# A two-layer hybrid decoder trunk on one core: first weights on another queue, and the outputs of four attention heads one step later

## The chip, the core and the metric

The kernel runs on one core of one Trainium2 chip. Its engines work side by side, each on its own list of instructions in a fixed order: TensorE (PE) multiplies matrices, VectorE (DVE) and ScalarE (ACT) work on elements, and GpSimd (POOL) has almost nothing to do here. Transfers (DMAs) are started by an instruction on the queue of one engine. In the kernel before, nearly all of them stand on SyncE (SP). An instruction waits until what it reads is there and until what it overwrites has been read; everything behind it on its engine waits with it.

The metric is the time of one execution in microseconds (us). The kernel before took 1193.77 us, the median of three runs (1192.67 to 1194.18).

## What is computed

The reference takes x, 512 tokens of width 1024, in float32, through two layers. The change touches the first layer's attention alone, which is this, cut to what matters:

```
proj = rms_norm(x) @ w_in                       # q, k, v of 8 dilated heads and 4 differential heads
qa, ka, qb, kb = rms_norm(each head) * gain
oa = dilated_mixture_attention(qa, ka, va)      # 8 heads of 64, causal, with a bias by distance

# differential: two softmaxes per head, v of width 128
p = softmax(q @ k.T * 64**-0.5 - slope * distance)      # c = 0, 1, causal
attn = p[:, :, 0] - lam * p[:, :, 1]
ob = rms_norm(attn @ v, b_sub_norm) * (1 - lam_init)
x += concat(oa, ob) @ w_out
```

A causal convolution with a gated unit follows each layer's mixer, and the second layer's mixer is a gated linear recurrence. The changed kernel does not touch these.

## The kernel before, in words

**Products.** Every product is made of three matmuls, since each float32 operand is split into a rounded part and the rest: for weights `wh` (cast on ACT, line 104) and `wl` (subtraction on DVE, line 106), for activations `xh` and `xl` (lines 231 and 233).

**Attention as eight tiles.** The queries, keys and values of layer 0 come in eight tiles of 384 columns, tile n = 0 to 7 in the order of `ORDER`: n = 0 to 3 are the four differential heads (`attn_b`), n = 4 to 7 are pairs of dilated heads (`attn_a`). One tile's projection is 16 groups of six matmuls: four units u of weights, and in each unit four blocks b of 128 tokens (`group`, lines 348 to 350). A unit of weights is cast on ACT and subtracted on DVE into one of four buffers, two units ahead, so a cast waits until PE has last read what stood in its buffer.

**The order of the work is written by hand.** `line` holds the groups of all tiles, one after the other, and behind them 32 short steps of the output projection (`early_out`). The attention of tile n is cut into steps, and `PLACES` says behind which group each stands, counted from the end of the tile's own projection: `qk` (transposes of q and k, line 414), `sc` (scores in three batches: blocks 0 and 1, block 2, block 3, line 447), `tr` (transposes of the softmaxed rows, line 468), `out` (attention times v, lines 481 to 491) and, for the differential heads, `norm`. `LAST` does the same for the last tile. Place 27.3 stands behind the eleventh group of the tile after next, so the output of one head falls into the scores of the next. PE keeps this order exactly (`pe`). The order on ACT, DVE and SP is made by a scheduler from the program's dependences.

**The output of a differential head.** `out` (lines 567 to 576) is twelve matmuls into the bank `O`, a copy of it to `ob` (ACT, line 571), its square `obsq` (ACT, line 573), and the split of the square into `obh` (ACT, line 126) and `obl` (DVE, line 127). `norm` (lines 578 to 593) multiplies both by a matrix of 1/128 (PE, lines 129 and 130, tile `obms`), which gives the mean of the squares, and works out the normalised output. The rows of the next head's softmax run on the same two engines: line 458 on DVE (an operation of the tensor and the bias with a running minimum), line 461 on ACT (the exponential), and line 556 on ACT (the scaling by the row's sum, line 515 in a dilated head).

**The start.** `first_tile` loads four pairs of x and weights, each transfer on SP's queue (lines 306 and 307), the first pair in two halves. ACT makes `xh`, then `wh`; DVE makes `xl`, then `wl`; then PE starts. Behind these transfers SP loads the other parameters (line 308), the next weights (line 113) and three tables of distances (`dist_a`, `lnc`, `dist_b`, lines 257 to 259), from which DVE makes the heads' biases (line 432).

Of the kernel before, what the change touches and what calls it, by code (L numbers as in the profile page):

```python
# [12 lines left out]
F32 = mybir.dt.float32  # L13
# [6 lines left out]
P = 128  # L20
S = 512
# [6 lines left out]
NT = 8  # L28

ORDER = (4, 5, 6, 7, 0, 1, 2, 3)  # L30


BATCHES = ((0, 1), (2,), (3,))
PLACES = dict(qk=9, sc=(12, 14, 16), tr=(18.5, 20.7, 23.5, 25.2), step=1, out=27.3, norm=29)
LAST = dict(qk=7.5, sc=(9.8, 10.5, 11.2), tr=(12.7, 13.4, 14.2, 15), step=0.35, out=16.2, norm=18)

OUT_GROUP = 0.65
# [25 lines left out]
def trunk(  # L63
# [15 lines left out]
    nc = tc.nc  # L79
    V, A, T, G = nc.vector, nc.scalar, nc.tensor, nc.gpsimd  # L80
# [13 lines left out]
    def nm(s):  # L94
        uid[0] += 1
        return f"{s}{uid[0]}"

    def bank(s):
        return pa.tile([P, S], F32, tag="pa", name=nm(s))
# [119 lines left out]
    with ExitStack() as actx:  # L219
        ap1 = actx.enter_context(tc.tile_pool(name="ap1", bufs=1))  # L220
        ap2 = actx.enter_context(tc.tile_pool(name="ap2", bufs=2))
        smp = actx.enter_context(tc.tile_pool(name="smp", bufs=2))
# [4 lines left out]
        def x_split(raw, cs):  # L227
            for c in cs:
                src = raw[:, (c % 2) * S : (c % 2 + 1) * S]
                hi = xp.tile([P, S], F32R, tag=f"xh{c}", name=nm("xh"))  # L230
                last = A.activation(hi, src, AF.Copy, scale=col(C_ATTN_G + c))
                lo = xp.tile([P, S], F32R, tag=f"xl{c}", name=nm("xl"))
                V.scalar_tensor_tensor(lo, src, col(C_ATTN_G + c), hi.bitcast(F32), ALU.mult, ALU.subtract)
                xs.append((hi, lo))
            return last
# [62 lines left out]
        def first_tile():  # L298


            xr = [ap2.tile([P, 13 * P], F32, tag=("pth", "ptl")[u % 2], name=nm("xr"))[:, : 2 * S] for u in range(4)]
            wr = [rawp.tile([P, 2 * CW], F32, tag="raw", name=nm("raw")) for u in range(4)]
            for u in range(4):
                for j in range(2 if u == 0 else 1):
                    cx, cw = (slice(j * S, (j + 1) * S), slice(j * CW, (j + 1) * CW)) if u == 0 else (slice(None),) * 2
                    nc.sync.dma_start(xr[u][:, cx], xT[u][:, cx])
                    nc.sync.dma_start(wr[u][:, cw], w_att[ORDER[0], u][:, cw])
            nc.sync.dma_start(pt[:, KC:], par[:, KC:])
            units = []
            for u in range(4):  # L310
                if u:
                    x_split(xr[u], (2 * u, 2 * u + 1))
                    units.append(split(wr[u], 2 * CW))
                    with tc.issue_after(last.ins):
                        x_square(xr[u - 1], (2 * u - 2, 2 * u - 1))
                    continue
                wh = whp.tile([P, 2 * CW], F32R, tag="wh", name=nm("wh"))
                wl = wlp.tile([P, 2 * CW], F32R, tag="wl", name=nm("wl"))
                for j in range(2):
                    cw = slice(j * CW, (j + 1) * CW)  # L320
                    last = x_split(xr[0], (j,))
                    with tc.issue_after(last.ins):
                        last = A.copy(wh[:, cw], wr[0][:, cw])  # L323
                    V.tensor_tensor(wl[:, cw], wr[0][:, cw], wh[:, cw].bitcast(F32), ALU.subtract)
                units.append((wh, wl))
            x_square(xr[3], (6, 7))
            return units
# [94 lines left out]
        oT = {}  # L422

        def where(n):
            return LAST if n == NT - 1 else PLACES

        def head_bias(h):
            bt = ap2.tile([P, S], F32, tag="bias", name=nm("bias"))
# [64 lines left out]
        def pt_tiles():  # L493
            return (ap2.tile([P, 13, P], F32R, tag="pth", name=nm("pth")),
                    ap2.tile([P, 13, P], F32R, tag="ptl", name=nm("ptl")))
# [46 lines left out]
        def attn_b(n):  # L542

            p = ORDER[n]
            st = {}

            def sc(blocks):
                if blocks[0] == 0:
                    st["b"] = head_bias(4 + p)
                rows = products(tiles[n]["qk"], blocks)  # L550
                for i in blocks:
                    for c in range(2):
                        st[i, c] = softmax_row(rows[c, i], i, st["b"])
                        if c == 0:
                            e0, r0 = st[i, 0]
                            A.activation(e0, e0, AF.Copy, scale=r0)
                        else:
                            (e0, _), (e1, r1) = st[i, 0], st[i, 1]
                            V.tensor_tensor(r1, r1, lam, ALU.mult)
                            V.scalar_tensor_tensor(e0, e1, r1, e0, ALU.mult, ALU.add)  # L560

            def tr(i):
                if i == 0:
                    st["pt"] = pt_tiles()
                transposed(st[i, 0][0], i, *st["pt"])

            def out():
                o_ps = bank("O")
                pv(o_ps, tiles[n]["v"], *st["pt"])
                st["o"] = smp.tile([P, S], F32, tag="sq", name=nm("ob"))  # L570
                A.copy(st["o"], o_ps)
                sq = smp.tile([P, S], F32, tag="sm3", name=nm("obsq"))
                A.activation(sq, o_ps, AF.Square)
                hi = smp.tile([P, S], F32R, tag="sq", name=nm("obh"))
                lo = smp.tile([P, S], F32R, tag="t", name=nm("obl"), bufs=1)
                st["ms"] = mean_rows("obms", hi, sq, lo)

            def norm():
                o = st["o"]
                ps, products_of = st["ms"]  # L580
                products_of(pe)
                y = smp.tile([P, S], F32, tag="sm3", name=nm("oby"))
                A.activation(y, ps, AF.Ln, bias=epsb)
                A.activation(y, y, AF.Exp, scale=-0.5)
                t = smp.tile([P, S], F32, tag="sq", name=nm("obt"))
                V.tensor_tensor(t, y, y, ALU.mult)
                V.scalar_tensor_tensor(t, ps, EPS, t, ALU.add, ALU.mult)
                V.tensor_scalar(t, t, -0.5 * (1.0 - LAM_INIT), 1.5 * (1.0 - LAM_INIT), ALU.mult, ALU.add)
                V.tensor_tensor(y, y, t, ALU.mult)
                V.scalar_tensor_tensor(o, o, col(C_BS), y, ALU.mult, ALU.mult)  # L590
                hi, lo = o_tiles(p)
                A.copy(hi, o)
                V.tensor_tensor(lo, o, hi.bitcast(F32), ALU.subtract)

            at = where(n)
            steps = [(g, partial(sc, b)) for g, b in zip(at["sc"], BATCHES)]
            steps += [(g, partial(tr, i)) for i, g in enumerate(at["tr"])]
            return steps + [(at["out"], out), (at["norm"], norm)]


# [376 lines left out]
```

## Time and profile before

| | before |
|---|---|
| median of three runs | 1193.77 us |
| the profiled execution | 1195.96 us |
| its span, first to last instruction | 1194.1 us |
| PE busy | 1181.2 us (99%) |
| DVE busy | 811.4 us (68%) |
| ACT busy | 585.6 us (49%) |
| granted TensorE clock, mean | 1.000 |

The page's span is 1.9 us shorter than the profiled execution, and that execution was 2.2 us above the median. The span is cut into 40 slices of 29.9 us on the page; layer 0's attention fills the first seven of them, up to about 230 us. PE is busy nearly without a gap, so what can be won or lost is what PE waits, and a wait is found by asking the trace what PE waited for, and then what the engine that it waited for was doing.

### The profile page before, as it was taken

The numbers are of one execution on the slowest core, as the hardware profiler recorded it, in microseconds if no ns is written. First come the engines' busy times: TensorE is split into PE (matmuls) and PEld (weight loads), VectorE is DVE, ScalarE is ACT, GpSimd is POOL, SyncE is SP. The second block draws the span as 40 slices with busy tenths as digits, with TensorE's granted clock in tenths as the row PEclk, the third lists the DMA queues.
The fourth block names the chain that finished last, engine by engine and source line by source line (L and its number), as shares of the span: only waits on it lengthen the run. The fifth ranks groups of instructions, "written<-read, shape, count | busy, mean of one in ns | idle before, by whom it ended". The sixth has DMA issues, their size and how long they took to land.

```text
span 1194.1 us, 14625 instructions
## 1 busy us (share of the span) xinstructions
PE 1181.2 (99%) x5566; PEld 990.6 (83%) x5566; DVE 811.4 (68%) x1327; ACT 585.6 (49%) x951; POOL 0.7 (0%) x6
## 2 busy tenths in 40 slices
PE   8999999999999999999999999999999999999998
PEld 8988888788888888888888878888888888888887
DVE  6977888688777763577436888668777763677431
ACT  6667788765444432344225688454444441444220
POOL 0000000000000000000000000000000000000000
PEclk9999999999999999999999999999999999999999
DMA  7221222062323232323233313323232323333221
GB/s 255 68 79 54 67 67 71 19 211 89 106 89 106 89 106 88 106 89 106 88 106 102 111 36 124 106 89 102 92 101 94 100 94 95 100 95 100 92 85 54
DMA packets 33910, 114.31 MB, mean 96 GB/s; under 512 B 3888, under 2 KB 4656, under 8 KB 33840
## 3 DMA queue, kind: packets, MB, share of 16 engines
q1 hardware_dynamic: 33552, 113.24, 29.8%
q8 instruction: 44, 0.72, 0.3%
q14 instruction: 26, 0.21, 0.1%
q10 hardware_dynamic: 288, 0.14, 0.0%
HBM read 111.27 MB, written 2.10 MB: 95 GB/s over the span
## 4 chain that ended last, share of the span: by engine, by line
PE 83%; ACT 3%; DVE 2%; issue 0%; DVEq 0%
PE mm L120 26%; PE mm L121 26%; PE mm L122 26%; ACT sm L461 1%; PE pj L348 1%; PE pj L350 1%; PE pj L349 1%; PE pt L468 1%; ACT sm L515 1%; PE S L447 0%; PE O L489 0%; DVE u L865 0%; DVE sm L458 0%; PE qkt L414 0%; DVE cv L708 0%
## 5 line engine op out<-in xcount | busy, mean ns | idle before, releaser
L104 ACT CAST wh<-raw 128x1024 fp32r<-128x1024 f32 (+1 forms) x207 | 211.1, 1021 | 285.8 <-PE mm L121 256.8
L122 PE MATMUL mm<-xh,wl 128*128 128x512 f32 x896 | 348.6, 389 | 0.0
L121 PE MATMUL mm<-xl,wh 128*128 128x512 f32 x896 | 348.6, 389 | 0.0
L120 PE MATMUL mm<-xh,wh 128*128 128x512 f32 x896 | 348.6, 389 | 0.0
L106 DVE TENSOR_TENSOR wl<-raw,wh 128x1024 fp32r<-128x1024 f32 (+1 forms) x207 | 244.8, 1184 | 43.0 <-ACT wh L104 39.4
L120 PEld LDWEIGHTS mm<-xh,wh 128*128 128x128 f32 x896 | 168.2, 188 | 35.0
L121 PEld LDWEIGHTS mm<-xl,wh 128*128 128x128 f32 x896 | 168.2, 188 | 35.0
L122 PEld LDWEIGHTS mm<-xh,wl 128*128 128x128 f32 x896 | 168.2, 188 | 34.9
L708 DVE SCALAR_TENSOR_TENSOR cv<-us,pt,cv 128x511 f32<-128x511 f32 (+2 forms) x216 | 160.5, 747 | 3.5
L120 PE MATMUL mm<-fh,wh 128*128 128x512 f32 x384 | 149.4, 389 | 0.0
L121 PE MATMUL mm<-fl,wh 128*128 128x512 f32 x384 | 149.4, 389 | 0.0
L122 PE MATMUL mm<-fh,wl 128*128 128x512 f32 x384 | 149.4, 389 | 0.0
L704 DVE TENSOR_TENSOR us<-mm,rs 128x512 f32<-128x512 f32 x104 | 71.6, 688 | 93.9 <-PE mm L122 93.6
L740 DVE TENSOR_TENSOR h<-mm,h 128x512 f32<-128x512 f32 (+1 forms) x49 | 33.2, 680 | 141.4 <-PE mm L122 141.4
L348 PE MATMUL pj<-wh,xh 128*128 128x384 f32 x256 | 92.7, 362 | 2.5 <-ACT wh L323 2.5
L729 ACT CAST fh<-cv 128x512 fp32r<-128x512 f32 x48 | 29.8, 621 | 126.4 <-DVE cv L726 126.4
L350 PE MATMUL pj<-wl,xh 128*128 128x384 f32 x256 | 87.2, 341 | 0.0
L349 PE MATMUL pj<-wh,xl 128*128 128x384 f32 x256 | 87.2, 341 | 0.0
L706 ACT ACTIVATE cv<-us,pt 128x512 f32<-128x512 f32 x104 | 84.3, 813 | 0.9 <-DVE us L704 0.6
L120 PEld LDWEIGHTS mm<-fh,wh 128*128 128x128 f32 x384 | 72.1, 188 | 15.0
L122 PEld LDWEIGHTS mm<-fh,wl 128*128 128x128 f32 x384 | 72.1, 188 | 15.0
L121 PEld LDWEIGHTS mm<-fl,wh 128*128 128x128 f32 x384 | 72.1, 188 | 14.9
(202 smaller groups left out, 1238.6 us busy)
## 6 DMA issues: line engine op xcount, KB each, us to landing
raw<-in_w_up_dram SPq DMA_DIRECT2D x96, 512.0 KB, 3.5
raw<-in_w_dn_dram SPq DMA_DIRECT2D x48, 512.0 KB, 3.5
raw<-in_w_att_dram SPq DMA_DIRECT2D x31, 384.0 KB, 3.4
raw<-in_w_ri_dram SPq DMA_DIRECT2D x16, 512.0 KB, 3.5
raw<-in_w_ao_dram SPq DMA_DIRECT2D x8, 512.0 KB, 3.6
raw<-in_w_ro_dram SPq DMA_DIRECT2D x8, 512.0 KB, 3.5
raw<-in_xT_dram SPq DMA_DIRECT2D x4, 512.0 KB, 4.4
out_dram<-h SPq DMA_DIRECT2D x7, 256.0 KB, 2.0
```

Of the source, the lines that this page charges most:

```text
L104: A.copy(hi, src)
L106: V.tensor_tensor(lo, src, hi.bitcast(F32), ALU.subtract)
L120: order(T.matmul(out, wh, xh, start=first, stop=False))
L121: order(T.matmul(out, wh, xl, start=False, stop=False))
L122: return order(T.matmul(out, wl, xh, start=False, stop=last))
L348: pe(T.matmul(o, xs[k][0][:, tb], wh[:, cw], start=k == 0, stop=False))
L349: pe(T.matmul(o, xs[k][1][:, tb], wh[:, cw], start=False, stop=False))
L350: pe(T.matmul(o, xs[k][0][:, tb], wl[:, cw], start=False, stop=k == KC - 1))
L704: V.tensor_tensor(u, ps, state["rs"], ALU.mult)
L706: A.activation(c, u, AF.Identity, scale=col(wcol + (taps - 1) * stride), bias=col(bcol))
L708: V.scalar_tensor_tensor(c[:, d:], u[:, : S - d], col(wcol + (taps - 1 - d) * stride), c[:, d:], ALU.mult, ALU.add)
L740: V.tensor_tensor(h[m][:, t], ps[:, t], h[m][:, t], ALU.add)
```

## The change

It has four parts.

1. The weights of the first tile, five transfers, are issued on ACT's queue and not on SP's.
2. In `PLACES`, `out` goes from 27.3 to 28.4 and `norm` from 29 to 30.4: outputs of tiles n = 0 to 5 stand one group later, for the differential heads behind the first scores of the next head and not ahead of them. (The last `tr` goes from 25.2 to 25.5, which is behind the same group.)
3. The last but one tile (n = 6) gets places of its own, `LAST_BUT_ONE`, closer together, with its output at 24.6 and not at 27.3.
4. The tiles `obsq` and `oby` take other buffers: `obsq` the one of tag `o`, `oby` the one of tag `t`, where both stood in the two buffers of tag `sm3`, which are also those of the last block of the softmax.

```
-PLACES = dict(qk=9, sc=(12, 14, 16), tr=(18.5, 20.7, 23.5, 25.2), step=1, out=27.3, norm=29)
+PLACES = dict(qk=9, sc=(12, 14, 16), tr=(18.5, 20.7, 23.5, 25.5), step=1, out=28.4, norm=30.4)
+LAST_BUT_ONE = dict(qk=9, sc=(12, 13.7, 15.4), tr=(17.8, 19.6, 21.4, 23.2), step=0.8, out=24.6)
 LAST = dict(qk=7.5, sc=(9.8, 10.5, 11.2), tr=(12.7, 13.4, 14.2, 15), step=0.35, out=16.2, norm=18)
...
                     nc.sync.dma_start(xr[u][:, cx], xT[u][:, cx])
-                    nc.sync.dma_start(wr[u][:, cw], w_att[ORDER[0], u][:, cw])
+                    A.dma_start(wr[u][:, cw], w_att[ORDER[0], u][:, cw])
             nc.sync.dma_start(pt[:, KC:], par[:, KC:])
...
         def where(n):
-            return LAST if n == NT - 1 else PLACES
+            return {NT - 1: LAST, NT - 2: LAST_BUT_ONE}.get(n, PLACES)
...
                 A.copy(st["o"], o_ps)
-                sq = smp.tile([P, S], F32, tag="sm3", name=nm("obsq"))
+                sq = smp.tile([P, S], F32, tag="o", name=nm("obsq"), bufs=1)
                 A.activation(sq, o_ps, AF.Square)
...
                 products_of(pe)
-                y = smp.tile([P, S], F32, tag="sm3", name=nm("oby"))
+                y = smp.tile([P, S], F32, tag="t", name=nm("oby"), bufs=1)
                 A.activation(y, ps, AF.Ln, bias=epsb)
```

The inserted line shifts every later line of the changed kernel by one, so line 461 of the kernel before is line 462 there. The texts below use the numbers of the kernel before; the rows of the order after the change have the new ones.

**The first place is ACT at the start.** Before, its only transfer is that of the first eight columns of parameters.

```order
L160 DMA pt<-in_par_dram 128x8
L231 ACTIVATE xh_150<-xr_129,pt 128x512
L323 CAST wh_148<-raw_133 128x384
L231 ACTIVATE xh_156<-xr_129,pt 128x512
L323 CAST wh_148<-raw_133 128x384
```

With the change:

```order
L161 DMA pt<-in_par_dram 128x8
L308 DMA raw_133<-in_w_att_dram 128x384 x2
L308 DMA raw_134<-in_w_att_dram 128x768
L308 DMA raw_135<-in_w_att_dram 128x768
L308 DMA raw_136<-in_w_att_dram 128x768
L232 ACTIVATE xh_150<-xr_129,pt 128x512
L324 CAST wh_148<-raw_133 128x384
```

Five transfers stand ahead of the first `xh`. The program's waits give the fourth and the fifth of them one each: transfers report on eight counters in turn, and the ninth waits until the first one on its counter has landed. The fourth waits for the first half of x, the fifth for the parameters.

**The second place is DVE in the first tile,** where `wl_172` and `wl_190` are the weights of units 1 and 2, and `xl_182` and `xl_186` the activations of unit 2. Before:

```order
L106 TENSOR_TENSOR wl_172<-raw_134,wh_170 128x768
L245 TENSOR_TENSOR xacc_178<-xsq_174,xsq_176 128x512
L233 SCALAR_TENSOR_TENSOR xl_182<-xr_131,pt,xh_180 128x512
L233 SCALAR_TENSOR_TENSOR xl_186<-xr_131,pt,xh_184 128x512
L106 TENSOR_TENSOR wl_190<-raw_135,wh_188 128x768
```

With the change:

```order
L107 TENSOR_TENSOR wl_172<-raw_134,wh_170 128x768
L433 TENSOR_SCALAR bias_552<-dist_b 128x512
L246 TENSOR_TENSOR xacc_178<-xsq_174,xsq_176 128x512
L234 SCALAR_TENSOR_TENSOR xl_182<-xr_131,pt,xh_180 128x512
L234 SCALAR_TENSOR_TENSOR xl_186<-xr_131,pt,xh_184 128x512
L107 TENSOR_TENSOR wl_190<-raw_135,wh_188 128x768
```

The bias of the first head, which reads `dist_b` and stood 17 instructions further on, now stands ahead of unit 2. On SP the three tables moved up too: they stand right behind the parameters and ahead of the next tile's weights, and by the same eight counters the issue of `dist_b` waits until the weights of unit 1 have landed.

**The third place is ACT at the output of head n = 0,** in the scores of head n = 1; the outputs of n = 1 and 2 stand alike. Before:

```order
L571 COPY ob_849<-O_836 128x512
L573 ACTIVATE obsq_851<-O_836 128x512
L104 CAST wh_1039<-raw_1037 128x768
L126 CAST obh_853<-obsq_851 128x512
L461 ACTIVATE sm_880,sum_883<-sm_880,mx_881 128x128
L461 ACTIVATE sm_887,sum_890<-sm_887,mx_888 128x128
L366 COPY qkraw_922<-pj_706 128x256
L378 ACTIVATE v_923<-pj_706,rstd 128x128
L556 ACTIVATE sm_880<-sm_880,sum_883 128x128
```

With the change:

```order
L105 CAST wh_1039<-raw_1037 128x768
L462 ACTIVATE sm_858,sum_861<-sm_858,mx_859 128x128
L462 ACTIVATE sm_865,sum_868<-sm_865,mx_866 128x128
L557 ACTIVATE sm_858<-sm_858,sum_861 128x128
L462 ACTIVATE sm_873,sum_876<-sm_873,mx_874 128x256
L462 ACTIVATE sm_880,sum_883<-sm_880,mx_881 128x256
L557 ACTIVATE sm_873<-sm_873,sum_876 128x256
L572 COPY ob_901<-O_888 128x512
L574 ACTIVATE obsq_903<-O_888 128x512
L367 COPY qkraw_922<-pj_706 128x256
L379 ACTIVATE v_923<-pj_706,rstd 128x128
L127 CAST obh_905<-obsq_903 128x512
```

The cast of weights and six operations of the next head's first two blocks, which stood behind the split of the square, now stand ahead of the copy of the output. On PE the two `obms` matmuls stood one group behind the scores of blocks 0 and 1, with the output and one group ahead of these; now the scores come first, then the output, two groups, the scores of block 2, and `obms` right behind them. For the output of n = 3, which falls into the scores of a dilated pair, ACT has four scalings and not two ahead of `obh`, and a second pair of the copies of lines 366 and 378.

## Rows read from the trace of the kernel before

**Rows 1.** What PE waited for, over the whole span: total, times, longest.

```profile
PE O L483 <- DVE ptl L472: 2.6, 3, 1.0
PE pj L348 <- ACT wh L323: 2.5, 2, 2.3
...
PE pt L468 <- DVE o L531: 1.1, 2, 0.8
PE pt L468 <- DVE ptl L472: 1.0, 2, 0.8
```

**Rows 2.** Timeline of PE, first tile: start, duration, line, tiles, count, wait before and releaser.

```profile
8.95 0.69 PE L348 MATMUL pj<-wh,xh 128*128 128x384 f32 x1 [2.32 <-ACT wh L323]
...
19.32 0.33 PE L350 MATMUL pj<-wl,xh 128*128 128x384 f32 x1
```

**Rows 3.** Timeline of ACT at the start.

```profile
3.91 0.72 ACT L231 ACTIVATE xh<-xr,pt 128x512 fp32r<-128x512 f32 x1 [1.89 <-DMA pt<-in_par_dram]
...
8.39 0.51 ACT L323 CAST wh<-raw 128x384 fp32r<-128x384 f32 x1 [2.23 <-DMA raw<-in_w_att_dram]
...
10.93 0.81 ACT L104 CAST wh<-raw 128x768 fp32r<-128x768 f32 x1
```

**Rows 4.** Timeline of SP's queue: the issues of the transfers.

```profile
2.12 0.43 SPq L307 DMA_DIRECT2D raw<-in_w_att_dram  x1
...
16.88 0.43 SPq L259 DMA_DIRECT2D dist_b<-in_dist_dram  x1
```

**Rows 5.** Transfers issued in the first 20 us: count, KB each, median us to landing.

```profile
dist_b<-in_dist_dram SPq DMA_DIRECT2D x1, 256.0 KB, 3.8
```

**Rows 6.** Timeline of DVE in the first tile.

```profile
12.65 0.68 DVE L245 TENSOR_TENSOR xacc<-xsq,xsq 128x512 f32<-128x512 f32 x1
13.26 1.41 DVE L233 SCALAR_TENSOR_TENSOR xl<-xr,pt,xh 128x512 fp32r<-128x512 f32 x2
14.58 0.95 DVE L106 TENSOR_TENSOR wl<-raw,wh 128x768 fp32r<-128x768 f32 x1
```

**Rows 7.** Timeline of PE at the output of head n = 1, and of tile 6's last scores.

```profile
86.98 0.40 PE L482 MATMUL O<-pth,v 128*128 128x512 f32 x1
88.33 0.50 PE L483 MATMUL O<-ptl,v 128*128 128x512 f32 x1 [0.95 <-DVE ptl L472]
...
91.27 0.33 PE L447 MATMUL S<-qh,qh 64*128 64x128 f32 x2
...
93.71 0.50 PE L130 MATMUL obms<-obl,ones_r 128*128 128x512 f32 x1
...
217.89 0.45 PE L447 MATMUL S<-qh,qh 64*128 64x384 f32 x2
...
218.62 0.50 PE L120 MATMUL mm<-oh,wh 128*128 128x512 f32 x1
```

**Rows 8.** Timeline of ACT at the output of head n = 1.

```profile
90.26 0.59 ACT L571 COPY ob<-O 128x512 f32<-128x512 f32 x1 [4.32 <-PE O L484]
...
91.23 0.83 ACT L104 CAST wh<-raw 128x768 fp32r<-128x768 f32 x1
91.96 0.63 ACT L126 CAST obh<-obsq 128x512 fp32r<-128x512 f32 x1
93.91 0.40 ACT L461 ACTIVATE sm<-sm,mx 128x128 f32<-128x128 f32 x1 [1.32 <-DVE mx L458]
...
94.69 0.35 ACT L366 COPY qkraw<-pj 128x256 f32<-128x256 f32 x1
...
95.21 0.40 ACT L556 ACTIVATE sm<-sm,sum 128x128 f32<-128x128 f32 x1
...
95.99 0.36 ACT L366 COPY qkraw<-pj 128x256 f32<-128x256 f32 x1
```

**Rows 9.** Timeline of DVE at the same place.

```profile
92.98 0.68 DVE L127 TENSOR_TENSOR obl<-obsq,obh 128x512 fp32r<-128x512 f32 x1
93.58 0.28 DVE L458 CUSTOM_DVE_ANT_0 sm<-S,bias 128x128 f32<-128x128 f32 x1
```

More of the change, by code (lines that the diff above doesn't have):

```diff
@@ L33 @@
 BATCHES = ((0, 1), (2,), (3,))
-PLACES = dict(qk=9, sc=(12, 14, 16), tr=(18.5, 20.7, 23.5, 25.2), step=1, out=27.3, norm=29)
+PLACES = dict(qk=9, sc=(12, 14, 16), tr=(18.5, 20.7, 23.5, 25.5), step=1, out=28.4, norm=30.4)
+LAST_BUT_ONE = dict(qk=9, sc=(12, 13.7, 15.4), tr=(17.8, 19.6, 21.4, 23.2), step=0.8, out=24.6)
 LAST = dict(qk=7.5, sc=(9.8, 10.5, 11.2), tr=(12.7, 13.4, 14.2, 15), step=0.35, out=16.2, norm=18)
@@ L306, in first_tile @@
                     nc.sync.dma_start(xr[u][:, cx], xT[u][:, cx])
-                    nc.sync.dma_start(wr[u][:, cw], w_att[ORDER[0], u][:, cw])
+                    A.dma_start(wr[u][:, cw], w_att[ORDER[0], u][:, cw])
             nc.sync.dma_start(pt[:, KC:], par[:, KC:])
@@ L424, in where @@
         def where(n):
-            return LAST if n == NT - 1 else PLACES
+            return {NT - 1: LAST, NT - 2: LAST_BUT_ONE}.get(n, PLACES)
         def head_bias(h):
@@ L571, in out @@
                 A.copy(st["o"], o_ps)
-                sq = smp.tile([P, S], F32, tag="sm3", name=nm("obsq"))
+                sq = smp.tile([P, S], F32, tag="o", name=nm("obsq"), bufs=1)
                 A.activation(sq, o_ps, AF.Square)
@@ L581, in norm @@
                 products_of(pe)
-                y = smp.tile([P, S], F32, tag="sm3", name=nm("oby"))
+                y = smp.tile([P, S], F32, tag="t", name=nm("oby"), bufs=1)
                 A.activation(y, ps, AF.Ln, bias=epsb)
```

## The prediction

> **What bounds the kernel now.** I read the page first: PE is busy 99% of the span (the table above), so only a wait of PE can be won, or a new one added. The list of PE's waits [rows 1] gives the places that this change can reach: 2.6 us in three outputs of differential heads (PE waits for the rest of the last transposed row, line 472), 2.5 us at the start for the first weights (line 323), 1.1 us twice at the end of layer 0's attention (a transpose that waits until DVE has read the output bank of tile 6, line 531), and 1.0 us in two transposes behind the banks of line 472. That is 7.2 us in all, 0.6% of the time. A measurement of this kernel can tell about 0.2%, 2.4 us, from no change. I then read the timelines at the start [rows 2 to 6] and at one output [rows 7 to 9].
>
> The start: PE stops for 2.32 us ahead of 8.95 [rows 2], because ACT waits 2.23 us for the second half of the first weights [rows 3]. That half was issued at 2.12 [rows 4] and was there only at 8.39, 6.3 us later, though SP had issued only three transfers ahead of it: it shares the engines with all that SP issues behind it.
>
> **The change part by part.**
>
> *The weights on ACT's queue.* Removed are five issues of some 0.43 us from SP; added are five ahead of ACT's first `xh`. Before, that one starts at 3.91 when the parameters have landed [rows 3]. Now ACT must first issue five transfers, and the last two of them wait until the first half of x and the parameters have landed. So the first `xh` comes about 2 issues later, 0.9 us by the 0.43 of one [rows 4]. This costs nothing in itself: what PE has after three matmuls is a wait of 2.32 us, which takes it up. How early the second half now lands no row shows. As bounds I take 6.3 us after an issue at about 1.6, which is 8.0 (a little earlier than 8.39), and on the other side the whole wait gone, 2.3 us.
>
> Whatever unit 0 wins must pass unit 2. On DVE the first head's bias now stands ahead of `xacc`, the two `xl` of unit 2 and its `wl`. It waits for `dist_b`. Before, that was issued at 16.88 and took 3.8 us [rows 4, 5]. Now its issue waits until the weights of unit 1 have landed; before, ACT cast these at 10.93 [rows 3], and the bytes ahead of them are about the same, so I set the issue at 11 to 12.5. With 3.8 us it lands at 14.8 to 16.3, and with two other tables, the parameters and the last weights beside it, perhaps at 17.5. From there it is 0.61 for `xacc` (13.26 − 12.65), at most as much for the bias, which is of the same size, 1.32 for the two `xl` (14.58 − 13.26) and 0.95 for `wl` [rows 6], 3.5 us. So unit 2's `wl` is done at 18.3 to 19.8, at worst 21.0. PE reads it first at 19.32 [rows 2]. So the gain that unit 0 makes is cut to at most 1.0 us, and a late table costs up to 1.7. I take **0** for the whole start, between the two; the ends are −1.0 and +1.7, and −2.3 if the table is so early that it does not hold DVE.
>
> The trace shows 6.3 us for a transfer that SP issued fourth, while the issue itself took 0.43 [rows 4]. The Trainium skill, page "DMA: Bandwidth & Descriptors", section "Issuing engines are not separate DMA queues", says that transfers run on the same 16 engines whoever started them, and that issuing from several engines saves only the time of the issue. By that rule the second half would come at most two issues earlier, and this part would be worth at most 0.9 us; the row, with 0.43 of 6.3 us in the issue, agrees.
>
> *The outputs one group later.* PE's path, for the outputs of n = 0, 1, 2. Before, from the output's first matmul to the second `obms` it is 93.71 − 86.98 = 6.73 us, of which 0.95 is the wait for `ptl` [rows 7]. In it are the output, two groups and the scores of blocks 0 and 1. Now the scores come ahead of the output, so `ptl` has 0.9 us more and this wait goes. The stretch from the scores to the second `obms` holds the same work and the scores of block 2 as well, 218.62 − 217.89 = 0.73 us [rows 7]. Without any wait that is 6.73 − 0.95 + 0.73 = 6.51.
>
> But `obms` now hangs on ACT. The cast of weights begins when PE has last read its buffer, as the scores begin (91.23 and 91.27) [rows 7, 8]. From the cast to the first operation of line 461 it was 93.91 − 91.23 = 2.68, with `obl` on DVE between, which takes 93.58 − 92.98 = 0.60 [rows 8, 9] and is now not there: 2.08. Then come, ahead of the copy `ob`, two of line 461 (94.69 − 93.91 = 0.78), lines 556 and 461 (95.99 − 95.21 = 0.78), and once more 461 and 556, which I set at 0.85, a little over, as both have 256 columns: 2.41. Then lines 571 and 573 (91.23 − 90.26 = 0.97), 366 and 378 (95.21 − 94.69 = 0.52), and `obh`, 0.63, all [rows 8]. Sum: 2.08 + 2.41 + 0.97 + 0.52 + 0.63 = 6.61. `obl` takes 0.68 [rows 9] and PE starts about 0.05 after it: 7.34 after the cast, 7.3 after the scores began. PE wants it at 6.51. So a **new wait of 0.8 us** stands at `obms`. Net against before: n = 0, which has no wait before (three of the four outputs have one), +0.8; n = 1 and n = 2, where about 0.95 goes, −0.15 each.
>
> For n = 3 the next head is a dilated pair. ACT has two more scalings ahead of `obh` (at most 0.40 each, the duration of such a row [rows 8]; I take 0.35, so 0.7) and a second pair of lines 366 and 378 (0.52): 1.2 us more, 8.5 against 6.5. The wait there was 2.6 less the two of 0.95, so 0.7 [rows 1]: **+1.3**. But PE is then 1.3 later at transposes of this pair which wait for DVE 0.8 us today [rows 1], while DVE's rows are not held by `obms`. So 0.8 comes back, −0.8. Sum of the heads: 0.8 − 0.3 + 1.3 − 0.8 = **+1.0**. The ends: if the walk along ACT is 0.8 too long, the waits at `obms` shrink to 1.2 in n = 3 alone, and the sum is 1.0 − 4 × 0.8 = −2.2. If it is 0.5 too short, +3.0.
>
> *The last but one tile.* Its output now stands ahead of tile 7's scores, so DVE has read the bank before the transposes come: the two waits of line 531, 1.1 us, go [rows 1]. The closer transposes may wait 0.3 more for the bank of one another, as one of 0.25 does today (1.0 less 0.8) [rows 1]. I take **−1.0**, between −1.3 and −0.5.
>
> *The buffers.* `obsq` and `oby` no longer share with the softmax's last block. None of PE's waits is put down to that [rows 1], so nothing is won on PE. The square of the next tile (line 395) now waits for `obl`, and it is not on PE's path: 0.
>
> **The sum** is 0 + 1.0 − 1.0 = 0 against the profiled execution of 1195.96, which was itself 2.2 us above the median. Against the median, 1193.77, I say **1193.8**, no change that can be measured.
>
> **The rivals.**
>
> *A, the start wins.* The second half of the weights lands early and `dist_b` does not hold DVE: −2.3, or, with the heads at their lower half (−0.5) and −1.0 at the tail, −3.8 and 1190.0. For it: the wait of 2.32 is plain, and SP's queue is freed of five issues. Against it: DVE's order, and what SP's transfers take whoever issues them. Chance 0.14.
>
> *B, `obms` does not wait.* If DVE reaches the next head's rows sooner than in my walk, the exponentials come ahead and the heads give −2.2: with the tail −3.2, at 1190.6. For it: each step of the walk is taken from rows in which ACT also did other work. Against: ACT's order is fixed, and the cast at its head cannot begin sooner. Chance 0.16.
>
> *C, slower: `dist_b` holds DVE.* If it lands at 16.8 or later, unit 2's `wl` comes at 20.3 or later and PE waits 1.0 to 1.7 us there. It decides from 15.8 on (19.32 less 3.5); with the heads at +2.0 to +3.0 and the tail at −1.0, the sum is +2.5 to +3.5: 1196.3 to 1197.3. For it: the two other tables, the parameters and the last weights and x stand ahead of it. Against: before, DVE had it 3.8 us after its issue. Chance 0.22.
>
> The forecast has 0.48; its own range is 1191.8 to 1195.8. The range takes in A, B and C but for their far ends: 1190.0 to 1197.0. Faster by over 0.2%: A and B for the most part, 0.27. Slower by over 0.2%: C and a little of the forecast's upper end, 0.23. Within: 0.50.
>
> **What would show it.** In the profile after: the wait of line 483 gone; one of line 129 or 130 for `obh` or `obl` (lines 126, 127) of some 0.8 in three heads and of 2 in the fourth; no wait for line 531; the first `xh` near 4.8; DVE idle for `dist_b` ahead of its bias. I am wrong if `obms` does not wait at all, if PE's idle time of the first 25 us shrinks by more than 1.0 us, or if unit 2 starts more than 1.7 us later than before.

## The result, and the profile after

The changed kernel took **1202.45 us**, the median of four runs (1201.46 to 1202.50), against 1193.45 us for the kernel before, the median of four runs beside it (1192.67 to 1194.18). The ratio is 1.0075, with an interval of 1.0063 to 1.0087: 9.0 us slower. The prediction said 1193.8 us and 1190.0 to 1197.0; the time lies 5.5 us above the range.

What PE waited for in the changed kernel (the columns are those of [rows 1]; line numbers are one higher):

```profile
PE obms L130 <- ACT obh L127: 4.2, 4, 2.1
PE pj L349 <- ACT wh L324: 2.8, 2, 1.9
PE pt L469 <- DVE ptl L473: 2.6, 2, 2.2
PE warm L616 <- DVE ones L169: 1.1, 1, 1.1
PE pj L351 <- DVE wl L107: 0.8, 1, 0.8
PE pr L122 <- DVE xrl L823: 0.7, 1, 0.7
PE obms L131 <- DVE obl L128: 0.7, 3, 0.2
PE qkt L415 <- DVE ptl L473: 0.5, 1, 0.5
```

The 2.6 us at the outputs [rows 1] are gone, and so are the two waits for line 531. In their place stand 4.9 us at `obms` and 2.2 us at a transpose. All waits of PE sum to 13.4 us here and to 7.7 us in the second profile of the kernel before that is used below, 5.7 us less, and so a part of the 9 is not a wait. It shows in the clock that TensorE was granted, at the start (first experiment) and at two more places. Rows of PE's timeline at these two:

```profile
149.02 0.70 PE L130 MATMUL obms<-obh,ones_r 128*128 128x512 f32 x1 [2.11 <-ACT obh L127]
149.82 0.80 PE L131 MATMUL obms<-obl,ones_r 128*128 128x512 f32 x1
150.42 0.52 PE L349 MATMUL pj<-wh,xh 128*128 128x384 f32 x1
150.74 0.52 PE L350 MATMUL pj<-wh,xl 128*128 128x384 f32 x1
...
152.80 0.34 PE L351 MATMUL pj<-wl,xh 128*128 128x384 f32 x1
152.97 0.34 PE L349 MATMUL pj<-wh,xh 128*128 128x384 f32 x1
...
233.57 0.88 PE L469 MATMUL pt<-ident,sm 128*128 128x128 f32 x6 [2.25 <-DVE ptl L473]
```

and the busy times by stretch there (the stretch, its length, the busy time of PE, PE's weight loads, DVE, ACT and POOL with the number of instructions, then the granted clock, 1.00 for 2.4 GHz and 0.50 for 1.2 GHz, the DMA share and GB/s):

```profile
145.00:149.00 4.00, 1.91 (x13) 1.34 (x11) 1.65 (x6) 3.97 (x12) 0.00 (x0) 1.00 0.14 56
149.00:152.00 3.00, 2.88 (x7) 2.28 (x8) 1.69 (x6) 2.71 (x7) 0.00 (x0) 0.52 0.02 5
...
153.00:157.00 4.00, 4.00 (x25) 3.30 (x24) 2.97 (x8) 3.94 (x11) 0.00 (x0) 1.00 0.01 2
...
234.00:238.00 4.00, 4.00 (x18) 3.25 (x16) 2.12 (x5) 1.45 (x3) 0.00 (x0) 0.57 0.00 0
```

Behind each of these two waits PE ran at 1.2 GHz for some 3.5 us: a projection matmul follows the one before after 0.32 us there, and after 0.17 us once the clock is back.

**Where the time went, stage by stage.** For this I take a second profile of the kernel before (first experiment; its span is 1191.4 us, and the 1200.7 of the changed kernel is 9.3 us longer). The landmarks on PE are the first transposes of q and k of a tile, and the last matmul of the last output. First the kernel before, then the changed one:

```profile
34.83 1.03 PE L414 MATMUL qkt<-ident,qkraw 128*128 128x128 f32 x8
132.37 0.82 PE L414 MATMUL qkt<-ident,qkraw 128*128 128x128 f32 x6
159.71 1.03 PE L414 MATMUL qkt<-ident,qkraw 128*128 128x128 f32 x8
208.38 1.04 PE L414 MATMUL qkt<-ident,qkraw 128*128 128x128 f32 x8
231.84 0.28 PE L489 MATMUL O<-pth,v 128*128 128x128 f32 x1
```

```profile
38.42 0.82 PE L415 MATMUL qkt<-ident,qkraw 128*128 128x128 f32 x6
136.45 0.82 PE L415 MATMUL qkt<-ident,qkraw 128*128 128x128 f32 x6
165.40 0.82 PE L415 MATMUL qkt<-ident,qkraw 128*128 128x128 f32 x6
215.07 0.60 PE L415 MATMUL qkt<-ident,qkraw 128*128 128x128 f32 x4
241.21 0.27 PE L490 MATMUL O<-pth,v 128*128 128x128 f32 x1
```

| stage | before, second profile | after | difference | forecast |
|---|---|---|---|---|
| start, to the first landmark | 34.83 | 38.42 | +3.6 | 0 |
| outputs of heads n = 0, 1, 2 (to 132.37 and 136.45) | 97.54 | 98.03 | +0.5 | +0.5 |
| output of head n = 3 (to 159.71 and 165.40) | 27.34 | 28.95 | +1.6 | +0.5 |
| dilated pairs, tile 6's transposes (to 208.38 and 215.07) | 48.67 | 49.67 | +1.0 | 0 |
| tail, to the last output | 23.46 | 26.14 | +2.7 | −1.0 |
| sum | | | +9.4 | 0 |

In the fourth row some 0.5 us is work and no loss: the changed places put two transposed rows (seven transposes of line 468) more ahead of the landmark, and as many fewer into the tail. So the tail itself lost some 3.2 us, by two new waits (2.25, and 0.53 at the transposes of q and k) and the lower clock, less the two waits for line 531. Of the start's 3.6 us, 2.4 are waits (3.66 in three against 1.25 in two). Behind the last output both kernels take the same time.

### The profile page after: what moved, and what is told of

Its sections match the earlier page's. It is cut to its first block, busy times and chain, and to the rows that moved or that the text cites. A ratio compares the mean times of both kernels' runs of the same rounds, so it can differ in the third digit from the quotient of the medians.

```text
span 1200.7 us, 14619 instructions
## 1 busy us (share of the span) xinstructions
PE 1183.3 (99%) x5566; PEld 993.4 (83%) x5566; DVE 812.9 (68%) x1327; ACT 585.9 (49%) x951; POOL 0.7 (0%) x6
## 4 chain that ended last, share of the span: by engine, by line
PE 91%; ACT 5%; DVE 2%; DMA 1%; issue 0%; DVEq 0%; SPq 0%
PE mm L123 26%; PE mm L122 26%; PE mm L121 26%; PE pj L349 3%; PE pj L350 3%; PE pj L351 3%; ACT sm L462 1%; DMA raw<-in_w_att_dram 1%; PE pt L469 1%; PE S L448 1%; ACT sm L516 1%; PE qkt L415 1%; DVE wl L107 1%; ACT wh L105 0%; PE O L490 0%
```

## The experiments

### Start: the profile that the prediction used was a slow start

A second run of the kernel before, with no edit.

> The kernel before, unchanged, for a second profile of it: the profile shown of it took 1195.96 us where other executions took 1192.7 to 1194.2. Theory (the difference is in the start): PE's wait ahead of the second half of the first weights, 2.32 us in the profile shown, is 0 to 1 us here, the span is near 1191.7 us, and every landmark behind the start (the transposes of q and k at 37.58, 59.01, 83.56 us) comes earlier by the same 2 to 2.4 us. Rival (it lies elsewhere, or outside the span): the start takes what it took and the landmarks stand where they stood.

Measured: 1193.60 us against 1193.65 (ratio 1.0002, 0.9992 to 1.0011), and a span of 1191.4 us. The theory held. ACT at the start:

```profile
3.67 0.72 ACT L231 ACTIVATE xh<-xr,pt 128x512 fp32r<-128x512 f32 x1 [1.65 <-DMA pt<-in_par_dram]
...
5.05 0.72 ACT L231 ACTIVATE xh<-xr,pt 128x512 fp32r<-128x512 f32 x1 [0.26 <-DMA xr<-in_xT_dram]
6.45 0.51 ACT L323 CAST wh<-raw 128x384 fp32r<-128x384 f32 x1 [0.67 <-DMA raw<-in_w_att_dram]
```

The second half of the weights was there at 6.45 and not at 8.39 [rows 3], and PE waited 0.9 us for it and not 2.3 [rows 2]. The landmarks came 2.75 us earlier throughout. Of that, 1.3 us are PE's waits (2.54 in two against 1.25 in two, without the first 1.1 us, line 615's, that every profile has). The rest is the clock: in the profile that the prediction read, matmuls follow each other after 0.32 us until 13.3 us, in the second profile after 0.17 to 0.19 us already from 7.9 us on, until the next wait. Two rows of PE's timeline in the first, two in the second:

```profile
9.44 0.52 PE L349 MATMUL pj<-wh,xl 128*128 128x384 f32 x1
9.76 0.52 PE L350 MATMUL pj<-wl,xh 128*128 128x384 f32 x1
```

```profile
8.05 0.34 PE L349 MATMUL pj<-wh,xl 128*128 128x384 f32 x1
8.23 0.35 PE L350 MATMUL pj<-wl,xh 128*128 128x384 f32 x1
```

In eight profiles with all these weights on SP's queue, in the order of before, the first landmark stood at 33.75 to 37.58 us, mean 35.4, and the one that the prediction read was the latest of the eight.

Then the change with the weights back on SP, and the kernel before with only this part of the change:

```
-                    A.dma_start(wr[u][:, cw], w_att[ORDER[0], u][:, cw])
+                    nc.sync.dma_start(wr[u][:, cw], w_att[ORDER[0], u][:, cw])
```

> The changed kernel with the first tile's weights on SP's queue again. Theory (start, heads and tail each cost their own part): the wait for dist_b on DVE goes, the start stands as in the kernel before; the time falls by 0.8 us if the start of the profile shown is typical, by about 3 us if that start was a slow one: 1199.4 to 1201.7 us. Rival (a late start only shifts what would wait anyway): the first wait at obms and the waits of the tail grow by what the start wins, and the time stays at 1202.4 us within 0.4.

> The kernel before with the first tile's weights on ACT's queue and nothing else. Theory (dist_b in front of unit 2's operands on DVE, and a later first xh): the first transposes of q and k come at 36.8 to 38.4 us, against 33.8 to 37.6 in three profiles with the weights on SP, and the time is 1195.0 to 1197.2 us. Rival (only the issue's time moves): within 0.9 us of the kernel before, 1192.8 to 1194.5.

Measured: 1197.81 us for the first, 4.6 less than the changed kernel, which is more than expected; and 1196.45 us for the second (ratio 1.0022, 1.0012 to 1.0032), 2.5 us more than before, as the theory had it. The first landmark stood at 33.75 without the part and at 37.90 with it alone. In six profiles with all five transfers on ACT it stood at 36.79 to 38.51, mean 37.9: **2.5 us later** than with SP. PE's waits ahead of the landmark sum to 3.2 us in the mean on ACT and to 1.2 on SP, so 2.0 of the 2.5 us are waits. In the profile without the part the tail, too, is 1.6 us shorter, by the clock (below); whether that is the rest of the 4.6 in its other runs was not shown.

What makes the start late? ACT's timeline in the changed kernel, and then DVE's:

```profile
1.19 4.35 ACTq L308 DMA_DIRECT2D raw<-in_w_att_dram  x5
5.58 0.72 ACT L232 ACTIVATE xh<-xr,pt 128x512 fp32r<-128x512 f32 x1 [3.57 <-issue]
...
8.68 0.51 ACT L324 CAST wh<-raw 128x384 fp32r<-128x384 f32 x1 [1.35 <-DMA raw<-in_w_att_dram]
```

```profile
16.75 0.43 DVE L433 TENSOR_SCALAR bias<-dist_b 128x512 f32<-128x512 f32 x1 [3.99 <-DMA dist_b<-in_dist_dram]
...
19.02 0.95 DVE L107 TENSOR_TENSOR wl<-raw,wh 128x768 fp32r<-128x768 f32 x1
```

Three things are late. The first `xh` comes at 5.58, since the five issues last until 5.54. The second half of the weights comes at 8.68. And DVE is held by `dist_b` for 3.99 us, so that unit 2's `wl` starts at 19.02 and PE waits 0.83 us for it. To part the first two, only the first pair's two halves went on ACT's queue; then no issue there waits for a landing, and DVE has the bias where it was:

```
+                    (A if u == 0 else nc.sync).dma_start(wr[u][:, cw], w_att[ORDER[0], u][:, cw])
```

> The kernel before with only the first pair's two halves of weights on ACT's queue; the order on DVE then has the bias behind the weights of the next tile, as before, and no transfer on ACT waits for another to land. Theory: no wait of DVE for dist_b, and the second half of the weights as early as before or earlier; time 1192.0 to 1193.7 us. Rival (it is the transfers that stand ahead of the first xh on ACT that cost): 1194.5 us or more.

Measured: 1196.54 us (ratio 1.0021, 1.0011 to 1.0030), so the theory fell, and the whole cost stayed. The time is where the rival put it, but not for the rival's reason: the first `xh` was at 4.28, against 3.67 to 4.07 in the eight profiles on SP, yet the second half of the weights was cast at 8.49 and PE waited 2.25 us for it. The late half is what costs; neither ACT's five issues nor `dist_b` is needed for it. The transfers themselves show it. These rows are the first two transfers of weights, in the second profile of the kernel before and in the changed kernel (count, size, median us from issue to landing); the row with the pair on ACT reads as the second:

```profile
raw<-in_w_att_dram SPq DMA_DIRECT2D x2, 192.0 KB, 3.5
```

```profile
raw<-in_w_att_dram ACTq DMA_DIRECT2D x2, 192.0 KB, 5.4
```

On SP's queue it was 3.4 to 3.8 us in six profiles and 4.3 and 4.6 in two; on ACT's, 4.9 to 5.5 in seven. On SP's queue the second half stands ahead of the 512 KB of unit 1's x, and in the eight profiles there it lands 1.3 to 2.7 us ahead of them (in the second profile it was issued at 2.12 and took 4.3 us, the x at 2.59 and 6.6). On ACT's queue nothing keeps it ahead: in the seven profiles there it lands 0.2 to 0.6 us behind that x, though it was issued earlier than before (with the pair on ACT, at 1.67 and 6.8 us to land, the x on SP at 1.65 and 6.6). So it shares the engines with the x. To test that without a second queue, the kernel before with the order on SP changed:

```
-x[0] first half, w[0] first half, x[0] second half, w[0] second half, x[1], w[1], ...
+x[0] first half, w[0] first half, x[0] second half, x[1], w[0] second half, w[1], ...
```

> The kernel before, all on SP's queue, with the 512 KB of x for unit 1 issued ahead of the second half of the first weights. Theory (what the change costs at the start is that the second half of the weights no longer has a place in the queue ahead of the large transfers, so that it shares the engines with them): the second cast of line 323 starts at 7.5 to 8.5 us instead of 6.1 to 6.5, PE waits over 2 us, the first transposes of q and k come at 36.5 to 38.4 us and the time is 1195 to 1197 us. Rival (it is ACT's queue or ACT's issue that makes them late, whatever the order of the bytes): the cast at 6.1 to 6.8 us and 1193.2 to 1194.5 us.

Measured: 1196.18 us (ratio 1.0019, 1.0010 to 1.0028); the second cast at 8.71, the first landmark at 38.01. The time and the landmark came as in the theory, the cast a little later than its 7.5 to 8.5. ACT's order changed too, and put one `xh` of unit 1, which waited for its x until 8.08, ahead of that cast. But the half itself, issued at 2.59, took 6.0 us and landed at 8.55, so the `xh` can account for 0.2 us of the 8.71 at most. So 512 KB ahead of this half cost 2.2 us, which the measurement can't tell from the 2.5 of ACT's queue.

### Outputs of the differential heads

The change with `PLACES` as before:

```
-PLACES = dict(qk=9, sc=(12, 14, 16), tr=(18.5, 20.7, 23.5, 25.5), step=1, out=28.4, norm=30.4)
+PLACES = dict(qk=9, sc=(12, 14, 16), tr=(18.5, 20.7, 23.5, 25.2), step=1, out=27.3, norm=29)
```

> The changed kernel with PLACES as before (out 27.3, norm 29, last transposes 25.2). Theory (ACT's row operations ahead of the copy of the output hold obms back): no wait at obms, the waits of 0.95, 0.94 and 0.66 us at the output's second matmul come back, no lower clock behind the fourth head; time 1200.2 us, 2.2 less. Rival (the buffers of obsq and oby, not the places, hold the outputs back): obms still waits 0.5 us or more, and the time falls by less than 1 us.

Measured: 1201.51 us, 0.9 less than the changed kernel; the two intervals overlap, so that alone can't be told from no change, and more than half of the expected gain was missing. The waits at `obms` went, as the theory had it, and 2.3 us at the outputs' second matmul came back. The two stages of the heads' outputs took 97.37 and 27.24 us, 2.4 less than in the changed kernel, about the expected gain. But tile 6's transposes now waited 3.00 us (0.37 in the changed kernel), and tile 6's stage, from its landmark to tile 7's, took 2.6 us more; those of tile 7 waited 2.24. The parts are not independent: in both runs that have the denser last but one tile without the dilated pairs' later outputs these 3.00 us stand.

The places alone, without the buffers and the rest, and the buffers alone:

> The kernel before with the changed PLACES and nothing else. Theory (heads +2.1 us, the dilated tiles' outputs +0.8 by the seventh transposes, the last tile -0.4): 1196.1 us, with waits at obms of 0.9 us three times and 2.1 once. Rival (the two buffers that obsq and oby left are part of it): waits at obms above 1.2 us, or new waits at the scores of block 3, and 1198 us or more.

```
-                sq = smp.tile([P, S], F32, tag="sm3", name=nm("obsq"))
+                sq = smp.tile([P, S], F32, tag="o", name=nm("obsq"), bufs=1)
...
-                y = smp.tile([P, S], F32, tag="sm3", name=nm("oby"))
+                y = smp.tile([P, S], F32, tag="t", name=nm("oby"), bufs=1)
```

> The kernel before with the changed buffers of obsq and oby and nothing else. Theory (where the outputs stand before, these buffers are free in time): no change, 1193.2 to 1194.4 us. Rival (the square of line 395 then waits for obl and delays the next tile's normalisation): 1195 us or more.

> The changed kernel with obsq and oby in the two buffers of the softmax's last block again. Theory (with the outputs one group later these buffers are still held when the next head's last block wants them, so that the transposes wait for the softmax, as in the run of the places alone): three waits of some 2.2 us of line 468 for line 560, a larger wait at the fourth obms, the lower clock behind them; 11 us more than the changed kernel: about 1213 us. Rival (the 14 us of the places alone came from something else, such as the common output places of the last tiles): 1204 us or less.

Measured: the places alone 1208.00 us (ratio 1.0126, 1.0109 to 1.0143), 14 us more; the buffers alone 1193.63 us (ratio 1.0000, 0.9991 to 1.0009); the change without the buffers 1212.37 us, 9.9 more than with them. So a part that is worth nothing by itself is worth 10 us beside another. PE's waits with the places alone:

```profile
PE pt L468 <- DVE sm L560: 6.8, 3, 2.4
PE obms L129 <- ACT obh L126: 5.2, 4, 3.1
```

and DVE in front of the first of these waits (the transposes start at 85.17):

```profile
79.17 0.75 DVE L590 SCALAR_TENSOR_TENSOR ob<-ob,pt,oby 128x512 f32<-128x512 f32 x1
...
81.30 0.68 DVE L458 CUSTOM_DVE_ANT_0 sm<-S,bias 128x512 f32<-128x512 f32 x1
...
84.37 0.74 DVE L560 SCALAR_TENSOR_TENSOR sm<-sm,sum,sm 128x512 f32<-128x512 f32 x1
```

By the program, line 458 writes the second row of the last block at 81.30 into a buffer that `oby` holds until line 590 has read it, from 79.17 on; between the two DVE does two other operations without a gap. With the outputs a group later the norm's chain runs into that row; with other buffers for `obsq` and `oby` it doesn't.

**A place where the later output pays.** The differential heads' outputs at 28.4, their norm two groups later than in the change, and the changed buffers; all else as before:

```
-PLACES = dict(qk=9, sc=(12, 14, 16), tr=(18.5, 20.7, 23.5, 25.2), step=1, out=27.3, norm=29)
+PLACES = dict(qk=9, sc=(12, 14, 16), tr=(18.5, 20.7, 23.5, 25.2), step=1, out=27.3, outb=28.4, norm=32.4)
...
-            return steps + [(at["out"], out), (at["norm"], norm)]
+            return steps + [(at["outb"], out), (at["norm"], norm)]
```

> The kernel before with the outputs of the differential heads at 28.4, their norm at 32.4 (behind the scores of block 3, two groups later than in the change), and the changed buffers; the dilated heads' places, the start and the tail as before. Theory (ACT needs 0.9 us more in three heads and 2.1 in the fourth, and PE's two groups and a batch of scores cover that): no wait at obms, none at the output's second matmul, 2.6 to 3.3 us less than before: 1190.4 to 1191.0 us. Rival (the row operations ahead of the copy push something else, the pth casts or v, onto PE's path): 1192.5 us or more.

Measured: **1190.82 us** (ratio 0.9975, 0.9966 to 0.9985), 3.2 us less than before, as expected. What PE waited for:

```profile
PE pt L468 <- DVE ptl L472: 2.4, 2, 2.2
PE warm L615 <- DVE ones L168: 1.1, 1, 1.1
PE pt L468 <- DVE o L531: 1.1, 2, 0.8
PE pj L348 <- ACT wh L323: 0.8, 2, 0.4
```

Neither the outputs nor `obms` wait. What is left is 2.2 us at the first dilated pair's transposes. The last run goes for that, and for the waits for line 531: the transposes of n = 4 at 20.5, 22.2, 24 and 25.7, and those of the last tile and its outputs 0.7 later.

> The kernel with the differential heads' outputs at 28.4, their norm at 32.4 and the changed buffers (it took 1190.8 us), and with two more edits: the transposes of the first dilated pair (n = 4) 0.5 to 2 groups later, so that they do not wait for ACT, and the last tile's transposes and outputs 0.7 group later. Theory: the wait of 2.17 us at the first dilated pair goes, those of 0.25 and 0.80 us for line 531 go in part: 1188.0 to 1189.0 us, 5 us less than the kernel before. Rival (ACT is behind for that whole tile, and the wait moves to the next transposes or to the output): 1190 us or more.

Measured: 1190.19 us (ratio 0.9971, 0.9959 to 0.9983). So the theory's 1188.0 to 1189.0 us was missed, and the time is where the rival put it. The wait of 2.2 us went and this tile took 25.43 us and not 27.51, but the next one took 26.70 and not 25.54, with two new waits for line 472 of 0.27 and 0.23 us in it; the tail stayed at 23.5. The interval overlaps that of the run before, so the two further edits gained nothing that can be told from noise.

### The last but one tile

The change with the last but one tile at the common places, and with only its outputs moved back:

```
-            return {NT - 1: LAST, NT - 2: LAST_BUT_ONE}.get(n, PLACES)
+            return LAST if n == NT - 1 else PLACES
```

> The changed kernel with the last but one tile at the common places (out at 28.4). Theory (the tail's 3.7 us come from tile 6's outputs standing ahead of tile 7's scores, while tile 7's transposes stay where they are): the wait of 2.25 us at tile 7's transposes goes and the clock stays at full speed behind it; time 1198.7 us, 3.7 less than the changed kernel, or up to 1 us more than that since two waits for line 531 of 1.05 us come back. Rival (the tail is short of time on ACT whatever the order, as the places of the other tiles moved too): the wait stays above 1.5 us and the time above 1201 us.

```
-LAST_BUT_ONE = dict(qk=9, sc=(12, 13.7, 15.4), tr=(17.8, 19.6, 21.4, 23.2), step=0.8, out=24.6)
+LAST_BUT_ONE = dict(qk=9, sc=(12, 13.7, 15.4), tr=(17.8, 19.6, 21.4, 23.2), step=0.8, out=27.3)
```

> The changed kernel with the outputs of the last but one tile back at 27.3 (behind tile 7's scores), its transposes and scores as dense as in the change. Theory (tile 7's scores stand two outputs and a step later while its transposes stay, so ACT has 4 us less for its softmax): the wait of 2.25 us and the lower clock behind it go, two waits for line 531 come back, from the seventh transposes of q and k to the last output 23.0 to 23.8 us instead of 26.1, time 1199.0 to 1200.5 us. Rival (the denser transposes of tile 6 themselves press on ACT and DVE): 25 us or more there, and 1201.5 us or more.

Measured: 1199.23 and 1199.18 us, 3.2 and 3.3 less than the changed kernel. From the last landmark (tile 7's, "the seventh" of the texts here) to the last output it was 23.07 and 23.43 us; the changed kernel takes 26.14 there and the kernel before 23.46. So the place of the outputs is what the tail lost by. The denser transposes take some 0.5 us of work out of this stretch and add a wait of 0.53 us at tile 7's transposes of q and k (line 415), which about cancels. How it comes about is seen on ACT in the changed kernel, from tile 7's softmax to its first transposed rows:

```profile
224.95 0.40 ACT L462 ACTIVATE sm<-sm,mx 128x128 f32<-128x128 f32 x1 [1.09 <-DVE mx L459]
...
231.72 1.32 ACT L516 ACTIVATE sm<-sm,sum 128x512 f32<-128x512 f32 x2
232.95 0.94 ACT L472 CAST pth<-pt 128x128 fp32r<-128x128 f32 x4
```

Tile 7's scores start at 222.54, behind both outputs of tile 6. ACT then needs eight microseconds, without a gap, for their exponentials and scalings, and in its order the casts of the transposed rows stand behind all of them. PE comes to the transposes at 228.41, fills its banks and waits until 233.57.

The part alone:

> The kernel before with the denser last but one tile and nothing else. Theory (the tail's cost is its own and needs none of the other parts): 1.1 to 2.7 us more behind the seventh transposes of q and k, by whether the clock falls after the wait, none ahead of them; 1195.1 to 1196.8 us. Rival (it only hurts because the outputs of the dilated pairs moved too): within 0.5 us of the kernel before.

Measured: 1199.85 us (ratio 1.0052, 1.0037 to 1.0067), 6.1 us more than before. The sign was right, the size too small and the place wrong: the theory had nothing ahead of the last landmark, and there the whole cost stands. Tile 6's stage took 29.38 us against 23.14, the tail 23.81 against 23.46, in spite of its wait of 2.25 us, behind which the clock did not fall here. Without the later outputs of the dilated pairs PE waits 3.00 us at tile 6's own transposes, as in the change without its places, and here the clock falls with it as well (0.70 and 0.62 in the two stretches of 5 us from 205 us on).

### The clock

No run was made for it alone, but the same wait stands in several profiles with and without what follows. In the changed kernel the wait of 2.25 us in the tail is followed by 1.2 GHz, and the tail takes 26.14 us. With the weights on SP the same wait, 2.27 us, is followed by this:

```profile
230.00:234.00 4.00, 4.00 (x26) 3.28 (x25) 2.49 (x5) 1.87 (x4) 0.00 (x0) 1.00 0.00 0
```

and the tail takes 24.57 us. So the lower clock cost **1.6 us** there, beside a wait of 2.25. The wait at the fourth head's `obms`, 2.11 us in the changed kernel, is 2.12 with tile 6's outputs moved back; there the clock is still at 0.50 from 152 to 155 us, where the changed kernel has it back at 152.6, and this stage took 30.29 us and not 28.95. Between the start and the end of the attention, every wait of 0.5 to 1.1 us was followed by full speed in all sixteen profiles. Of the twenty waits of 2.1 to 3.1 us in them, fourteen were followed by the lower clock and six were not. What tells the six from the fourteen stays open.

## Why the prediction was wrong

*The walk along ACT at the outputs held.* It gave 7.34 us from the cast of the weights to the second `obms`; the changed kernel has the cast at 89.84 and `obms` at 97.23, 7.39. The wait forecast at 0.8 was 0.92 (0.69 and 0.23) in three heads. In the fourth it gave 8.5 us, and it was 149.82 − 140.93 = 8.9. The net of the first three, forecast at +0.5, was +0.5. The gain of 0.8 us at the transposes of the dilated pair came too. ACT's rows there, with the columns of [rows 8], and the row of PE at their end:

```profile
89.84 0.83 ACT L105 CAST wh<-raw 128x768 fp32r<-128x768 f32 x1 [2.11 <-PE pj L350]
...
95.84 0.62 ACT L127 CAST obh<-obsq 128x512 fp32r<-128x512 f32 x1
...
97.23 0.50 PE L131 MATMUL obms<-obl,ones_r 128*128 128x512 f32 x1 [0.23 <-DVE obl L128]
```

*The fourth head was mis-sized by 1.1 us,* since a wait of 2.11 us was priced as 2.11 us. The half clock behind it was in no term, though the profile of before shows the same at the start, where matmuls follow each other after 0.32 us behind the wait at 8.95 (the rows at 9.44 and 9.76 above).

*The start failed twice.* The step "I take **0** for the whole start" set the second half of the weights between 8.0 and 8.39, or earlier, on ACT's queue. It was 7.5 to 8.9 there, so that was nearly right. But the comparison was with a profile in which that half was at 8.39 on SP's queue too, where it is at 6.1 to 6.8 in six profiles of eight. The prediction noted that this profile stood 2.2 us above the median and that the start held a wait of 2.32 us, and did not put the two together: the excess of the profiled run stood at the start, about half of it in that wait and half in the slower matmuls around it. Nor does its reason for the late half, that it shares the engines with all that SP issues behind it, explain the 6.3 us: the same transfers stood behind it in the second profile, where it took 4.3. The second failure was the direction. The lower end of the term was a gain of 2.3 us, the upper end a loss of 1.7 from `dist_b`; that a transfer on another queue may lose its turn was no case. The rule cited in the prediction (the Trainium skill, page "DMA: Bandwidth & Descriptors", section "Issuing engines are not separate DMA queues") also says that such transfers interleave whatever engine started them, and the landings, 4.9 to 5.5 us against mostly 3.4 to 3.8, agree. I worked out only what its half about the issue would save.

*Rival C's mechanism was there:* `dist_b` landed at 16.75, and unit 2's `wl` was done 3.2 us later against 3.5 in the working. PE waited 0.83 us. But it was not what decided, as the pair on ACT's queue costs the same without it.

*The tail was the wrong sign.* The step said that tile 6's output "now stands ahead of tile 7's scores, so DVE has read the bank before the transposes come", −1.0. The two waits of line 531 did go. What the step left out is the other side of the same exchange: the scores stand behind the outputs now, and the transposes that need them did not move. ACT's eight microseconds for tile 7's softmax were not walked. They cost 2.25 us of waiting, and 1.6 of clock where it fell.

*The signs did not watch the right places.* None of the three signs of being wrong came: `obms` waited, PE's idle time of the start did not shrink, and PE read unit 2's `wl` 0.7 us later (20.02 against 19.32). They compared with the slow start, and none stood at the tail.

*The buffers at 0* was right only in the sense that no wait of the kernel before was theirs. Beside the later places they are worth 10 us, and without them the change would have been at 1212.

## What to carry to other kernels

When a step is moved ahead of another, walk what the other one's consumers now have left, not only what the moved step wins. Before pricing a wait from one profile, ask whether that run was above the median by about the size of that wait; a second profile of the same kernel settles it. And on a kernel whose PE is busy 99% of the time, price a new wait of two microseconds twice, without and with a fall of the clock behind it (here 2.25 us, and 1.6 us more), or put more work ahead of the step that would wait, as the norm at 32.4 does.

## What the runs showed of the hardware

The first two transfers of weights, 192 KB each, took 4.9 to 5.5 us to land (the median of the two, seven profiles) when they were issued from a queue of their own beside another queue's large ones, and 3.4 to 3.8 us in six of eight profiles (4.3 and 4.6 in two) when they stood ahead of these in the same queue. The second of them was issued earlier, at 1.67 and not at 2.12, and yet landed at 7.5 to 8.9 us and not at 6.1 to 6.8 (7.5 and 8.4 in the two).

Behind a wait of about 2 to 3 us PE was mostly, but not always (fourteen times of twenty), granted 1.2 GHz for some 3 to 7 us, at the same place of the same program once with it and once without (26.14 and 24.57 us for the same tail). At the start matmuls followed each other after 0.32 us, as at 1.2 GHz, for some 3 to 6 us behind the wait for the second half of the weights in thirteen of the sixteen profiles; the other three have the three earliest landmarks (33.75, 34.16 and 34.83). In five of the thirteen the clock reads 1.00 in that stretch all the same, as here for the kernel before:

```profile
9.00:13.00 4.00, 4.00 (x13) 3.91 (x14) 3.05 (x5) 3.75 (x7) 0.00 (x0) 1.00 1.02 406
```

In these five traces the first record of the clock stands at 12.6 to 13.9 us, so the 1.00 ahead of it is no reading; there the pitch of the rows is the better witness.
